# A hybrid diffusion layer on one core: the merge and the up-projection in hand-laid order on four engines

## The chip, the cores and the metric

One core of a Trainium2 chip runs the whole layer as one program. The metric is the device time of one execution, in microseconds (us). The engines are called as the profile calls them: PE (TensorE's matmuls; PEld its weight loads), DVE (VectorE), ACT (ScalarE), POOL (GpSimd) and SP (SyncE, which issues the DMAs here). Each engine takes its own instructions strictly in order, so an instruction that waits holds up all that stand behind it on that engine.

## The reference, cut to what matters

A layer with attention and a state-space part is followed by a merge and a feed-forward part. The change touches what follows after the attention output `attn` and the state-space output `ssm` are there:

```python
x = x + gate1 * (concat([rms_norm(attn, g_attn), rms_norm(ssm, g_ssm)]) @ w_out)   # the merge
h = rms_norm(x, g_norm2) * (1 + scale2) + shift2
up = h @ w_up                       # 1024 -> 5632 features
acc = conv3(up, conv_w) + conv_b    # centred, along the tokens, per feature
g, val = split(acc, 2)
x = x + gate2 * ((silu(g) * val) @ w_down)
y = rms_norm(x, g_final)
```

There are 128 prompt tokens and 2048 sample tokens, 2176 together (17 tiles of 128). All data are float32.

## The kernel before, in words

**Precision.** A float32 operand is split in two: ACT writes a rounded copy (hi), DVE or POOL subtracts it from the operand (lo), and three products hi·hi, hi·lo, lo·hi stand for one. So each operand of a matmul costs an ACT copy and a subtraction.

**The merge** (`merge`, L1016, in a loop over the 17 token tiles with two more passes of the loop behind them). The state-space half of each tile is turned by PE into the bank `to` and split into `oT` (`turned`, L974: copy L981, subtraction L982, square and sum L238 over `to`). 24 matmuls (tile `pm`, L280) are scaled, gated and added to x on DVE and POOL (`merge_ssm`, L1084 to L1086). `h2_begin` (L1092) takes the sum of squares of the finished row (ACT, L238), makes 1/rms on POOL (L239, L241) and scales to `xn` (DVE, L1109). In the next pass of the loop `h2_end` (L1112) turns `xn` into the banks `tp` (L1118), applies scale and shift with eight ACT instructions (L1121) and, for tokens from number 726 on, stores the result from the staging tile `stg` (two buffers) to the DRAM tensor `hd` (L1132). The square at L238 needs a place for its unused result, and `h2_begin` gives it the very `stg` tile that L1121 fills later. The last tile also clears six columns of its `stg` (MEMSET, L1106).

From pass 8 on the merge also prepares the feed-forward part: sums of token quarters on POOL (`sums0`, L1058), the split of token operands (`split_tokens`, L1181 copy, L1182 subtraction) and the first seven weight operands (`up_operands`, L1210 sums on POOL, L1215 copy, L1216 subtraction).

**The up-projection** (`ffn_up`, L1222) multiplies 2x2 blocks with seven products instead of eight. It makes three passes c = 0, 1, 2 over the tokens (726 each), each pass over 22 feature blocks fb, so 66 units. A unit has seven products of 12 matmuls of 366 columns: product 0 of the unit (the first one, `begin`, L1266, made ahead in the unit before), 1 into bank `Y`, 2 into `X`, 3 into `Z`, 4 into `X`, then product 0 of the next unit, 5 into `X`, 6 into `Z`. Between them ACT takes snapshots of the running bank `X` (`snap`, L1263: s1 before product 2, s2 before 4, s3 before 5), DVE adds snapshots to other banks (L1307, L1320, L1332), and the convolution is three taps (`taps`: ACT L1245, DVE L1246, L1247) on each of four results g1, v2, v1, g2. `silu` is an ACT tanh (L1253) and a DVE instruction (L1254); POOL multiplies (L1258, tile `th`) and SP stores to `ffd`. Meanwhile the weight operands of the next unit are made one by one (`step`): in pass 0 four sums on POOL, seven copies on ACT, six subtractions on DVE and one on POOL; in the passes 1 and 2 four of the seven come back from DRAM (`wsd`). `combos` makes the token combinations of the next pass on POOL; `operand` loads and splits them, two in unit fb = 18 and five in unit fb = 21.

**What sets the order.** Inside `tc.manual_schedule` an engine keeps the order of the code; elsewhere a scheduler chooses it by its own timeline. The merge is manual on PE, ACT, DVE and POOL, `ffn_up` on PE and POOL alone; SP is never manual here.

The down-projection (`ffn_down`, L1369) follows, in two halves of 11 blocks; `down_tile` and `down_early` load and split its first operands during the last two up units.

## Time and profile before

| what | us |
|---|---|
| median of 3 runs (2651.84 to 2657.8) | 2655.93 |
| the profiled execution | 2655.35 |
| its span, first to last instruction | 2653.6 |
| input projection, attention, state space | 0 to 980 |
| merge, until the first product of the up-projection | 980 to 1161 |
| up-projection: pass 0, pass 1, pass 2 | 1161 to 1515, to 1824, to 2135 |
| down-projection | 2135 to the end |

PE is busy for 2426.5 us of the span (91%), DVE 1738.3 (66%), ACT 1320.4 (50%) and POOL 1103.0 (42%). The granted clock of TensorE is given as a share of full speed (2.4 GHz): 1.00 where all of a stretch was at that level, 0.5 where all was at 1.2 GHz, and a mean between them; over the whole span it is 0.96. The shares are averages over stages with different limits; a stage is read by itself. A busy PE is the best sign of a stage that PE sets, since nothing else in these stages has to be as long as PE's own work.

### The profile page before, as it was taken

To read this page: it belongs to the slowest core of one execution; us is meant where nothing else is said; L and a number is where in the kernel's file an instruction comes from. 1 tells how busy PE (TensorE), PEld (TensorE's weight loads), DVE (VectorE), ACT (ScalarE), POOL (GpSimd) and SP (SyncE) were. 2 spreads that over 40 slices of the span, in tenths; PEclk is the share of its full clock that TensorE was granted. 3 is DMA by queue.
4 is the path that set the end of the run, shared out by engine and by line. 5 is a ranking of instruction groups with operands and counts; after the bars stand their busy time and mean duration, and the time that the engine had idled before them with its cause. 6 is when DMAs were issued, how large, how long until landed. Compare 5 with 4: busy or idle time off the path is not lost.

```text
span 2653.6 us, 38068 instructions
## 1 busy us (share of the span) xinstructions
PE 2426.5 (91%) x13294; PEld 2146.2 (81%) x13294; DVE 1738.3 (66%) x2979; ACT 1320.4 (50%) x2626; POOL 1103.0 (42%) x1393
## 2 busy tenths in 40 slices
PE   6986997799999779769998899999999999999998
PEld 3765785688887557569898899999999988888887
DVE  6999776877777876668888865567556542224333
ACT  6643557777776566555555644445444430112111
POOL 2686304577677725546666522232222221111101
PEclk8988998899999889879999999999999999999999
DMA  7554755421111657756777787788766763334432
GB/s 243 172 162 159 210 145 150 133 67 66 66 64 65 124 178 241 225 158 236 250 250 268 281 279 250 263 290 291 243 233 228 247 212 119 117 125 146 126 115 75
DMA packets 291039, 482.63 MB, mean 182 GB/s; under 512 B 42025, under 2 KB 187553, under 8 KB 290721
## 3 DMA queue, kind: packets, MB, share of 16 engines
q1 hardware_dynamic: 285953, 471.30, 54.6%
q10 hardware_dynamic: 4896, 8.92, 1.0%
q8 instruction: 105, 1.72, 0.3%
q14 instruction: 85, 0.70, 0.1%
HBM read 323.82 MB, written 153.95 MB: 180 GB/s over the span
## 4 chain that ended last, share of the span: by engine, by line
PE 56%; DVE 8%; issue 6%; ACT 5%; POOL 5%; DMA 4%; SPq 0%; POOLq 0%; DVEq 0%; ACTq 0%
PE dn L280 19%; PE X L1239 14%; PE Z L1239 7%; PE Y L1239 3%; PE pt L1009 3%; PE ps L858 2%; DMA hd<-stg 2%; POOL S L1210 2%; PE pt L886 2%; DVE w L1216 1%; PE pm L280 1%; ACT stg L1121 1%; PE po L890 1%; PE po L891 1%; DVE pTl L897 1%
## 5 line engine op out<-in xcount | busy, mean ns | idle before, releaser
L1239 PE MATMUL X<-T,w 128*128 128x366 f32 x3168 | 561.3, 332 | 30.6 <-ACT s L1263 27.5
L1239 PEld LDWEIGHTS X<-T,w 128*128 128x128 f32 x3168 | 536.3, 190 | 39.2 <-ACT s L1263 33.9
L1258 POOL TENSOR_TENSOR th<-th,v 128x363 f32<-128x363 f32 x132 | 139.6, 1058 | 550.1 <-issue 230.2
L1239 PE MATMUL Z<-T,w 128*128 128x366 f32 x1584 | 287.1, 330 | 3.3 <-DVE Y L1320 3.3
L280 PE MATMUL dn<-dnw,T 128*128 128x512 f32 (+1 forms) x1242 | 288.9, 386 | 0.0
L1239 PEld LDWEIGHTS Z<-T,w 128*128 128x128 f32 x1584 | 268.6, 189 | 4.2 <-DVE Y L1320 4.2
L280 PEld LDWEIGHTS dn<-dnw,T 128*128 128x128 f32 x1242 | 231.0, 188 | 47.0
L1408 DVE TENSOR_TENSOR td<-dn,gate 128x512 f32<-128x512 f32 (+1 forms) x69 | 47.1, 684 | 300.6 <-PE dn L280 300.6
L280 PE MATMUL dn<-T 128*128 128x512 f32 (+1 forms) x828 | 196.4, 386 | 0.0
L1347 ACT ACTIVATE T<-stg 128x1408 fp32r<-128x1408 f32 x34 | 47.1, 1385 | 281.0 <-PE dn L280 274.2
L280 PEld LDWEIGHTS dn<-T 128*128 128x128 f32 x828 | 154.0, 188 | 31.3
L194 DVE SCALAR_TENSOR_TENSOR wacc<-wa,scf,wacc 128x256 f32<-128x256 f32 x224 | 164.4, 778 | 12.8 <-ACT wacc L196 7.4
L1239 PE MATMUL Y<-T,w 128*128 128x366 f32 x792 | 143.8, 331 | 0.0
L897 DVE TENSOR_TENSOR pTl<-pt,pTh 128x512 fp32r<-128x512 f32 x158 | 108.1, 684 | 50.2 <-ACT pTh L896 48.6
L1263 ACT ACTIVATE s<-X 128x366 f32<-128x366 f32 x198 | 94.0, 475 | 93.2 <-PE X L1239 92.4
L239 POOL TENSOR_SCALAR ssq<-ssq 128x1 f32<-128x1 f32 x68 | 24.0, 353 | 269.7 <-ACT xn L238 91.9
L1239 PEld LDWEIGHTS Y<-T,w 128*128 128x128 f32 x792 | 134.9, 190 | 0.0
L1215 ACT ACTIVATE w<-upraw 128x512 fp32r<-128x512 f32 x198 | 121.9, 624 | 22.7 <-PE Z L1239 18.5
L624 POOL TENSOR_TENSOR fm<-HS,A 128x544 f32<-128x544 f32 x64 | 93.3, 1459 | 94.9 <-DVE HS L606 79.3
L860 DVE CUSTOM_DVE_ANT_0 sm<-ps,mask,nsink 128x640 f32<-128x640 f32 (+2 forms) x136 | 112.7, 830 | 28.9 <-PE ps L858 28.6
L1409 POOL TENSOR_TENSOR xd<-xd,td 128x512 f32<-128x512 f32 x34 | 46.5, 1371 | 197.5 <-DVE td L1408 191.6
L847 ACT ACTIVATE sm<-sm,nm 128x640 f32<-128x640 f32 (+2 forms) x136 | 107.6, 791 | 26.4 <-DVE nm L860 25.9
(493 smaller groups left out, 5498.6 us busy)
## 6 DMA issues: line engine op xcount, KB each, us to landing
w<-wsd SPq DMA_DIRECT2D x176, 512.0 KB, 5.1
upraw<-in_w_up_dram SPq DMA_DIRECT2D x88, 512.0 KB, 5.8
wsd<-w SPq DMA_DIRECT2D x88, 512.0 KB, 4.7
ffd<-th SPq DMA_DIRECT2D x132, 181.5 KB, 2.2
stg<-ffd SPq DMA_DIRECT2D x34, 704.0 KB, 4.8
xd<-x1d SPq DMA_DIRECT2D x34, 512.0 KB, 4.8
wa<-in_w_ada_dram SPq DMA_DIRECT2D x64, 256.0 KB, 3.0
upraw<-in_w_up_dram SPq DMA_DIRECT2D x44, 256.0 KB, 4.2
```

Of the source, the lines that this page charges most:

```text
L194: V.scalar_tensor_tensor(o, raw[:, k % RK], g, o, op0=OP.mult, op1=OP.add)
L280: self.T.matmul(ps, lhs(a, k), rhs(b, k), start=(first and k == 0 and n == 0), stop=(last and k == nk - 1 and n == 2))
L624: e.tensor_tensor(m, ev[:, :, ::-1] if n else ev, A[n], op=OP.mult)
L847: S.activation(out[hh][:, :W], out[hh][:, :W], AF.Exp, scale=-1.0, bias=nm[:, hh:hh + 1], accum_out=l[:, hh:hh + 1])
L858: T.matmul(ps[:, c:c + n], qT[:, h, :], kt, start=(a == 0), stop=(a == 1))
L860: V.tensor_tensor_reduce(t[:, :W], ps[:, c0:c0 + W], mask, -1.0, self.nsink[:, h:h + 1], op0=OP.add, op1=OP.min, accum_out=nm[:, hh:hh + 1])
L897: V.tensor_tensor(lo, pv, hi, op=OP.subtract)
L1009: T.matmul(pm, oT[:, a, k, :], w[:, b, k, cs], start=(n == 0), stop=(n == 11))
L1215: S.activation(w[:, 0], x, AF.Copy)
L1239: self.T.matmul(bank[:, :NI], w[:, a, k], t[:, b, k, :NI], start=(first and k + n == 0), stop=(k == 3 and n == 2), skip_group_check=True)
L1258: G.tensor_tensor(th, th, v, op=OP.mult)
L1263: S.activation(s[:, :NI], x[:, :NI], AF.Copy)
```

## The change

It does six things.

1. `h2_begin` gives the square the tile `xn` as its place for the unused result, in place of `stg`.
2. `ffn_up` and the merge stand in one manual order on PE, ACT, DVE and POOL. The code of `ffn_up` is written in the order wanted: the taps and silu of a unit's last result (g2) move behind product 1 and 2 of the next unit (`late`, `th2`).
3. The first product of the up-projection is made inside the merge, into a bank `X` of a pool of its own (three banks, `xp`); `to` has one bank in place of two and `tp` two in place of four. The fourth sum of quarters and the fourth token operand move into the merge too.
4. Loads of token operands are issued one or two units ahead of their splits (`load`, `split`), and the splits are spread over the units fb = 19, 20, 21 and 0 of the next pass.
5. In the passes 1 and 2 the second half of each token subtraction goes to POOL.
6. The loads of the first down operands are likewise issued ahead (`down_load`, `down_fetch`).

```diff
 def turned:   ps = pp.tile([128, 4, 128], F32, name="to", bufs=2 -> 1)
 def h2_end:   ps = pp.tile([128, 4, 128], F32, name="tp", bufs=4 -> 2)
...
     def merge(self, w, p, pp, xp):
             if 1 <= i <= NT:
                 hs[i - 1] = self.h2_begin(i - 1, xs.pop(i - 1), p)
+            if i == NT:
+                x = xp.tile([128, 512], F32, name="X", bufs=3)
+                self.product(wts[0], toks[0, 0], x, True)
             if i >= 2:
                 self.h2_end(i - 2, *hs.pop(i - 2), pp)
-            if i in (9, 11):
-                toks.append(self.split_tokens(len(toks), self.quarter(0 if i == 9 else 2)))
-            if 10 <= i < 16:
-                self.sums0((i - 10) // 2, slice(2 * (i % 2), 2 * (i % 2) + 2))
-            if i == 14:
-                toks.append(self.split_tokens(2, self.quarter(0)))
+            if i in (9, 11, 13):
+                j = len(toks)
+                toks[0, j] = self.operand0(j)
+            if 8 <= i < 16:
+                self.sums0((i - 8) // 2, slice(2 * (i % 2), 2 * (i % 2) + 2))
+            if i == NT:
+                toks[0, 3] = self.operand0(3)
...
     def h2_begin(self, i, x1, p):
-        r = self.rstd(x1.rearrange("p (k c) -> p k c", k=8), D, p, h[:, :, 0:128])
+        r = self.rstd(x1, D, p, xn)
...
     def split_tokens(self, n, src):
-            self.V.tensor_tensor(t[:, 1, k:k + 2, :NI], src[:, k:k + 2], t[:, 0, k:k + 2, :NI], op=OP.subtract)
+            e = self.G if k and n > 6 else self.V
+            e.tensor_tensor(t[:, 1, k:k + 2, :NI], src[:, k:k + 2], t[:, 0, k:k + 2, :NI], op=OP.subtract)
...
     def ffn_up(self, first, p, pp, xp):
+        banks = {0: (x0, snap(x0, "s1"))}
+        for j in range(4, 7):
+            toks[0, j] = self.operand0(j)
         for u, (c, fb) in enumerate(units):
...
             product(u, 1, y, True)
+            if late:
+                g2 = late()
+            step()
             V.tensor_tensor(y[:, :NI], y[:, :NI], s1[:, :NI], op=OP.add)
             product(u, 2, x)
             s2 = snap(x, "s2")
+            if late:
+                th2(g2)
             g1 = taps(y, 0, fb, "g1")
             t1 = silu(g1, y)
+            step()
+            if fb == 21:
+                split(c + 1, 3)
+                load(c + 1, 5)
+            if fb == 0:
+                split(c, 5)
...
             product(u, 3, z, True)
+            step()
+            if fb == 19:
+                split(c + 1, 0)
+                load(c + 1, 2)
             product(u, 4, x)
             s3 = snap(x, "s3")
             V.tensor_tensor(y[:, :NI], z[:, :NI], s3[:, :NI], op=OP.add)
+            step()
+            if u + 1 < len(units):
+                x1 = xp.tile([128, 512], F32, name="X", bufs=3)
+                product(u + 1, 0, x1, True)
             v2 = taps(y, 1, fb, "v2")
...
             product(u, 6, z)
             V.tensor_tensor(z[:, :NI], z[:, :NI], s2[:, :NI], op=OP.add)
-            g2 = taps(z, 0, fb, "g2")
-            gated(silu(g2, z), v2, 2 * c + 1, fb)
+            def late(z=z, fb=fb):
+                return taps(z, 0, fb, "g2")
+            def th2(g2, z=z, v2=v2, c=c, fb=fb):
+                gated(silu(g2, z), v2, 2 * c + 1, fb)
...
-            with self.pool("mrg2") as p, self.pool("mps2", bufs=2, space=PSUM) as pp:
-                with tc.manual_schedule(engines={ET.PE, ET.Activation, ET.DVE, ET.Pool}):
-                    first = self.merge(w, p, pp)
-            with fx, self.pool("upc") as p, self.pool("upps", space=PSUM) as pp:
-                with tc.manual_schedule(engines={ET.PE, ET.Pool}):
-                    self.ffn_up(first, p, pp)
+            xp = fx.enter_context(self.pool("upx", space=PSUM))
+            with tc.manual_schedule(engines={ET.PE, ET.Activation, ET.DVE, ET.Pool}):
+                with self.pool("mrg2", side="right") as p, self.pool("mps2", bufs=2, space=PSUM) as pp:
+                    steps = self.merge(w, p, pp, xp)
...
+                with fx, self.pool("upc") as p, self.pool("upps", space=PSUM) as pp:
+                    self.ffn_up(first, p, pp, xp)
```

Three places show the order. Names are tiles; a number behind a name tells one buffer from the next, and `x8` means eight in a row. The first place is PE at the end of the merge, before:

```order
L280 MATMUL pm<-wo,oT 128x512 x24
L1118 MATMUL tp<-ident,xn 128x128 x24
L1239 MATMUL X<-T,w 128x366 x12
L1239 MATMUL Y<-T,w 128x366 x12
L1239 MATMUL X<-T,w 128x366 x12
```

and in the changed kernel:

```order
L280 MATMUL pm<-wo,oT 128x512 x24
L1126 MATMUL tp<-ident,xn 128x128 x8
L1197 MATMUL X<-T,w 128x366 x12
L1126 MATMUL tp<-ident,xn 128x128 x16
L1197 MATMUL Y<-T,w 128x366 x12
L1197 MATMUL X<-T,w 128x366 x12
```

The first product (X) stands ahead of the last two tiles' transposes. The second place is POOL in one unit of pass 0, before (S are the four sums for the next unit's weights, w the one subtraction, th the two last products of a unit: first that of v1, then that of v2):

```order
L1216 TENSOR_TENSOR w<-upraw,w 128x512
L1258 TENSOR_TENSOR th<-th,v_13875 128x363
L1258 TENSOR_TENSOR th<-th,v_13836 128x363
L1210 TENSOR_TENSOR S<-upraw 128x512
L1210 TENSOR_TENSOR S<-S,upraw 128x512
L1210 TENSOR_TENSOR S<-upraw 128x512
L1210 TENSOR_TENSOR S<-upraw,S 128x512
```

and in the changed kernel:

```order
L1231 TENSOR_TENSOR w<-upraw,w 128x512
L1262 TENSOR_TENSOR th<-th,v_13875 128x363
L1225 TENSOR_TENSOR S<-upraw 128x512
L1262 TENSOR_TENSOR th<-th,v_13849 128x363
L1225 TENSOR_TENSOR S<-S,upraw 128x512
L1225 TENSOR_TENSOR S<-upraw 128x512
L1225 TENSOR_TENSOR S<-upraw,S 128x512
```

The second product of `th` changes places with the first sum. The third place is DVE in one unit of pass 0, before:

```order
L1320 TENSOR_TENSOR Y<-Z,s_14617 128x366
L1246 SCALAR_TENSOR_TENSOR v_14625<-Y,vec,v_14625 128x363
L1247 SCALAR_TENSOR_TENSOR v_14625<-Y,vec,v_14625 128x363
L1216 TENSOR_TENSOR w<-S,w 128x512 x2
L1246 SCALAR_TENSOR_TENSOR v_14664<-X,vec,v_14664 128x363
L1216 TENSOR_TENSOR w<-S,w 128x512
L1247 SCALAR_TENSOR_TENSOR v_14664<-X,vec,v_14664 128x363
L1332 TENSOR_TENSOR Z<-Z,s_14583 128x366
L1216 TENSOR_TENSOR w<-S,w 128x512
L1216 TENSOR_TENSOR w<-upraw,w 128x512 x2
L1307 TENSOR_TENSOR Y<-Y,s_14642 128x366
```

and in the changed kernel, from the add of the last product of a unit on:

```order
L1374 TENSOR_TENSOR Z<-Z,s_14103 128x366
L1231 TENSOR_TENSOR w<-S,w 128x512
L1250 SCALAR_TENSOR_TENSOR g_14237<-Z,vec,g_14237 128x363
L1251 SCALAR_TENSOR_TENSOR g_14237<-Z,vec,g_14237 128x363
L1231 TENSOR_TENSOR w<-upraw,w 128x512
L1316 TENSOR_TENSOR Y<-Y,s_14174 128x366
L1258 SCALAR_TENSOR_TENSOR th<-Z,g_14237 128x363
L1250 SCALAR_TENSOR_TENSOR g_14266<-Y,vec,g_14266 128x363
L1251 SCALAR_TENSOR_TENSOR g_14266<-Y,vec,g_14266 128x363
L1258 SCALAR_TENSOR_TENSOR th<-Y,g_14266 128x363
L1231 TENSOR_TENSOR w<-upraw,w 128x512
L1231 TENSOR_TENSOR w<-S,w 128x512
```

The six subtractions of weights, which stood in one cluster, now stand one or two at a time between the taps.

## Rows read from the trace of the kernel before

**Rows 1.** Windows: merge, merge body, merge end, pass 0, pass 1; PE, PEld, DVE, ACT, POOL, clock, DMA.

```profile
989.40:1050.94 61.54, 61.54 (x319) 51.97 (x317) 44.70 (x62) 36.95 (x91) 34.98 (x53) 0.98 0.78 263
1050.94:1133.94 83.00, 58.35 (x252) 45.73 (x250) 51.91 (x59) 43.40 (x103) 43.29 (x49) 0.84 0.79 218
1133.94:1186.44 52.50, 33.88 (x145) 30.65 (x146) 33.58 (x38) 29.90 (x64) 21.27 (x18) 0.69 0.55 171
1186.44:1515.23 328.79, 303.12 (x1766) 295.59 (x1765) 277.34 (x405) 183.74 (x342) 209.07 (x160) 0.99 0.70 248
1530.00:1790.00 260.00, 260.00 (x1557) 260.00 (x1556) 155.65 (x283) 124.16 (x226) 77.77 (x73) 1.00 0.78 268
```

**Rows 2.** Waits in 980 to 1165: us in total, times, longest.

```profile
ACT stg L238 <- DMA hd<-stg: 40.1, 9, 7.6
...
POOL ssq L239 <- ACT stg L238: 24.8, 10, 8.4
```

**Rows 3.** Chain that ended last, 1040 to 1165: start, us, what.

```profile
1094.03 7.06 DMA hd<-stg
...
1102.40 2.79 ACT stg L1121 x8
...
1150.04 5.13 DMA hd<-stg
```

**Rows 4.** Timeline of one token in the merge body: start, us, engine, instruction, [idle before].

```profile
1083.23 0.68 DVE L982 TENSOR_TENSOR oT<-to,oT 128x512 fp32r<-128x512 f32 x1
...
1086.73 1.82 POOL L1086 TENSOR_TENSOR mx__12116<-mx__12116,p 128x512 f32<-128x512 f32 x1
...
1090.44 0.19 POOL L239 TENSOR_SCALAR ssq<-ssq 128x1 f32<-128x1 f32 x1 [1.89 <-ACT stg L238]
...
1091.26 1.73 POOL L1058 TENSOR_TENSOR T<-T 128x732 f32<-128x732 f32 x1
1091.33 2.21 DVE L1109 TENSOR_SCALAR xn<-mx__12024,rstd 128x1024 f32<-128x1024 f32 x1 [3.92 <-POOL rstd L241]
...
1093.88 1.75 DVE L1182 TENSOR_TENSOR T<-T 128x732 fp32r<-128x732 f32 x2 [0.34 <-ACT T L1181]
```

**Rows 5.** Timeline of PE at the end of the merge.

```profile
1133.94 8.01 PE L280 MATMUL pm<-wo,oT 128*128 128x512 f32 x24 [3.19 <-ACT to L238]
...
1158.28 1.94 PE L1118 MATMUL tp<-ident,xn 128*128 128x128 f32 x8 [7.27 <-DVE xn L1109]
...
1164.84 2.77 PE L1239 MATMUL Y<-T,w 128*128 128x366 f32 x12
1171.69 4.03 PE L1239 MATMUL X<-T,w 128*128 128x366 f32 x12 [4.08 <-ACT s L1263]
```

**Rows 6.** Groups by line on DVE, 1200 to 1500: count, busy, mean ns, idle before.

```profile
L1216 DVE TENSOR_TENSOR w<-S,w 128x512 fp32r<-128x512 f32 x76 | 92.2, 1237 | 13.9 <-ACT w L1215 13.3
L1216 DVE TENSOR_TENSOR w<-upraw,w 128x512 fp32r<-128x512 f32 x38 | 31.9, 860 | 0.0
```

**Rows 7.** The same groups in pass 1, 1530 to 1790.

```profile
L1216 DVE TENSOR_TENSOR w<-upraw,w 128x512 fp32r<-128x512 f32 x36 | 24.9, 692 | 0.0
```

**Rows 8.** Timeline in pass 0: POOL's sums beside DVE's subtractions.

```profile
1246.10 1.28 POOL L1210 TENSOR_TENSOR S<-upraw 128x512 f32<-128x512 f32 x1
...
1246.84 2.79 DVE L1216 TENSOR_TENSOR w<-S,w 128x512 fp32r<-128x512 f32 x2 [1.85 <-ACT w L1215]
...
1247.34 1.75 POOL L1210 TENSOR_TENSOR S<-upraw,S 128x512 f32<-128x512 f32 x1
```

**Rows 9.** Timeline in pass 0: DVE idle between taps and silu, behind ACT.

```profile
1237.56 0.60 DVE L1246 SCALAR_TENSOR_TENSOR g<-Y,vec,g 128x363 f32<-128x363 f32 x1 [0.23 <-ACT g L1245]
...
1239.70 0.54 DVE L1254 SCALAR_TENSOR_TENSOR th<-Y,g 128x363 f32<-128x363 f32 x1 [0.60 <-ACT Y L1253]
...
1243.13 0.60 DVE L1246 SCALAR_TENSOR_TENSOR v<-X,vec,v 128x363 f32<-128x363 f32 x1 [0.29 <-ACT v L1245]
```

**Rows 10.** Waits in 1165 to 1510: us in total, times, longest.

```profile
POOL th L1258 <- DVE th L1254: 76.8, 19, 5.0
...
PE X L1239 <- ACT s L1263: 26.4, 18, 4.1
```

More of the change, by code (lines that the diff above doesn't have):

```diff
@@ L1047, in merge @@
                 wts = next(more)
-        return toks, wts, more, raws
+        for _ in more:
+            pass
+        yield toks, wts, raws, x
     def quarter(self, m):
@@ L1264, in snap, with load, split @@
             return s
-        def begin(u):
-            x = pp.tile([128, 512], F32, name="X", bufs=3)
-            product(u, 0, x, True)
-            banks[u] = x, snap(x, "s1")
-        todo, raws = [], first[3]
-        begin(0)
+        banks = {0: (x0, snap(x0, "s1"))}
+        todo, late, th2 = iter(()), None, None
+        for j in range(4, 7):
+            toks[0, j] = self.operand0(j)
+        raw = {}
+        def load(c, *js):
+            if 0 < c < 3:
+                for j in js:
+                    raw[j] = self.load_tokens(c, j)
+        def split(c, j):
+            if 0 < c < 3:
+                toks[c, j] = self.split_tokens(7 * c + j, raw.pop(j))
         for u, (c, fb) in enumerate(units):
             x, s1 = banks.pop(u)
-            nxt = iter(())
+            nxt, down = iter(()), u + 2 - len(units)
             if u + 2 < len(units):
@@ L1283, in ffn_up @@
                 next(todo)
+            z = pp.tile([128, 512], F32, name="Z", bufs=3)
             y = pp.tile([128, 512], F32, name="Y", bufs=2)
-            z = pp.tile([128, 512], F32, name="Z", bufs=3)
-            refill = fb == 21 and c < 2
-            def step(j):
-                for w in (next(nxt, None),):
-                    if w:
-                        wts[u + 1] = w
-                if refill and j is not None:
-                    toks[c + 1, j] = self.operand(c + 1, j)
-            if fb == 18 and c < 2:
-                for j in range(2):
-                    toks[c + 1, j] = self.operand(c + 1, j)
@@ L1298, in ffn_up, with step @@
-            if c == 2 and fb in (18, 19):
-                self.down_in.append(self.down_tile(0, fb - 18))
-            down = u + 2 - len(units)
-            if down >= 0:
-                self.down_early(down)
-            product(u, 1, y, True)
+            def step():
+                w = next(nxt, None)
+                if w:
+                    wts[u + 1] = w
+            if fb == 18:
+                load(c + 1, 0, 1)
+                if c == 2:
+                    downs = [self.down_load(0, i) for i in range(2)]
@@ new lines, in ffn_up @@
+            if down == 0:
+                self.down_fetch(0, 1)
+            if down == 1:
+                self.down_fetch(2, 3)
+            product(u, 1, y, True)
+            if late:
+                g2 = late()
+            step()
+            V.tensor_tensor(y[:, :NI], y[:, :NI], s1[:, :NI], op=OP.add)
+            product(u, 2, x)
+            s2 = snap(x, "s2")
+            if late:
+                th2(g2)
+            g1 = taps(y, 0, fb, "g1")
+            t1 = silu(g1, y)
+            step()
@@ L1304, in ffn_up @@
+            if down == 0:
+                self.down_early(0)
             if down == 1:
                 self.down_early(2)
[L1306 to L1314 removed]
+                self.down_fetch(5)
+            product(u, 4, x)
+            s3 = snap(x, "s3")
@@ new lines, in ffn_up @@
+            V.tensor_tensor(y[:, :NI], z[:, :NI], s3[:, :NI], op=OP.add)
+            step()
+            if u + 1 < len(units):
+                x1 = xp.tile([128, 512], F32, name="X", bufs=3)
+                product(u + 1, 0, x1, True)
+            v2 = taps(y, 1, fb, "v2")
+            if u + 1 < len(units):
+                banks[u + 1] = x1, snap(x1, "s1")
+            if fb == 20:
+                split(c + 1, 2)
+                load(c + 1, 4)
+            if fb == 21:
+                split(c + 1, 4)
+                load(c + 1, 6)
@@ L1315, in ffn_up @@
+            if fb == 0:
+                split(c, 6)
             if down == 1:
@@ L1317, in ffn_up @@
                 self.down_early(4)
-            product(u, 4, x)
-            s3 = snap(x, "s3")
-            V.tensor_tensor(y[:, :NI], z[:, :NI], s3[:, :NI], op=OP.add)
-            step(4)
-            v2 = taps(y, 1, fb, "v2")
-            if u + 1 < len(units):
-                begin(u + 1)
-            step(None)
+            step()
             product(u, 5, x)
-            step(5)
+            step()
+            if fb == 19:
+                split(c + 1, 1)
+                load(c + 1, 3)
             v1 = taps(x, 1, fb, "v1")
```

102 lines of the change are left out of this document (52 added, 50 removed).

## The prediction

> **What bounds the kernel now.** The windows by stage come first [rows 1]. In a stage that PE sets, PE's busy time is the stage. So it is in the merge before its pass 8 (61.54 of 61.54 us, nine tokens of 36 matmuls, 6.84 us each) and in pass 1 of the up-projection (260.00 of 260.00). Pass 1 also gives PE's price of a unit: 260 us for 1557 matmuls, 0.167 us each, 84 to a unit: 14.03 us. Three stretches are not PE's: the merge body (83.00 us for 252 matmuls, seven tokens, 11.86 us each, clock 0.84), the merge end (52.50 us with 33.88 of PE, clock 0.69) and pass 0 (328.79 us for 1766 matmuls, 21 units, 15.66 us each). The change touches these three, so each is read for the wait that ends last in it.
>
> In the merge the waits name a loop through memory [rows 2]: ACT's square at L238 waits nine times, 40.1 us, for a store out of `stg`, because `stg` takes the square's unused result; POOL then waits 24.8 us for the squares. The chain that ended last shows the same loop [rows 3]: a store lands (7.06), L1121 fills the tile again (2.79), the next store. In the tail the store that counts lands at 1150.04 + 5.13 = 1155.17.
>
> In pass 0 DVE is busy 277.34 of 328.79 us and POOL 209.07 [rows 1], neither full. The groups by line show why DVE is still in the way: a subtraction w takes 1.237 us (from a sum S) or 0.860 (from a raw weight) [rows 6], and 0.692 in pass 1, where POOL does little [rows 7]. The timeline shows the difference being made [rows 8]: POOL's sum starts at 1246.10 and ends 1247.38, the first of two subtractions starts inside it, at 1246.84; the two take 2.79 us, and the second ends at 1249.63, 0.54 behind the sum that POOL ran from 1247.34 to 1249.09. So a subtraction of DVE and an operation of POOL do not run beside each other: whichever comes second waits. Also, POOL's `th` waits for DVE's silu 76.8 us in pass 0 [rows 10], with the four sums in order behind it.
>
> **The change, part by part.** The profiled execution took 2655.35 us (span 2653.6), 0.6 below the median; the sums below are against it. About 0.2%, 5.3 us, is what a measurement can tell from no change.
>
> *Merge body.* With the square's result in `xn`, the wait of 40.1 us [rows 2] has no cause left, since `xn` is read by PE and stored by nobody. Late next is the in-order loop of DVE and POOL. In the token shown [rows 4] `oT` starts at 1083.23, the x add ends at 1088.55, ssq starts at 1090.44 after 1.89 us of waiting for the square, and `xn` at 1091.33: 8.1 us after `oT`. Without the wait that is 6.2; then `xn` (2.21), partly beside sums of POOL (1.73), and one weight subtraction of 0.7 to 1.5: 9.1 to 9.9 us a token, and 1.75 more in the passes with a token split. Measured is 11.86. The gain is best counted by POOL's waits: 24.8 less the longest, 8.4, which is the tail's, leaves 16.4. Two more sums of quarters (2 x 1.73) now fall on passes 8 and 9; I let them cost 1.4, since POOL idles there. **15 us.** Ends: 8, if half the waits are taken over by x add and sums, and 35, if PE sets the tokens (83.00 - 7 x 6.84).
>
> *Merge end.* Before, the last `pm` ends at 1133.94 + 8.01 = 1141.95 and product 2 of the first unit starts at 1171.69 [rows 5]: 29.7 us, with 7.27 of waiting for `xn`, then the products, then 4.08 for a snapshot that ACT makes behind other work. Now the first product runs while the last tiles are being normalised, and its snapshot stands ahead of the splits of the last three token operands. What stays is a store: the last tile's MEMSET clears part of a `stg` buffer whose store must have landed, and on DVE `xn` is queued behind it. That path from the end of `pm`: transposes 1.0, eight of L1121 2.79, issue 0.3, store 5.13 [rows 3]: 9.2; then MEMSET and `xn`, before 3.1 from landing to transpose (1155.17 to 1158.28) and now at most that; transposes 1.0 to 1.94 [rows 5], L1121 2.79 again, of which half can overlap with PE's next product. About 16. **14 us**, ends 8 (the store takes 7.06 and the splits are in the way) and 18.
>
> *Pass 0.* POOL no longer holds all its sums behind the second `th`: the first sum goes ahead of it. What remains is DVE's own work plus its meetings with POOL. Busy is 277.34 / 21 = 13.2 a unit; of this 4 x (1.237 - 0.692) + 2 x (0.860 - 0.692) = 2.5 is waiting inside subtractions, so 10.7 is work. Idle behind ACT, between taps and silu, is 0.23 + 0.60 + 0.29 = 1.1 [rows 9] and stays. Laying the new order of DVE beside POOL's with these durations, I find four meetings: the subtraction from raw weights with `th` (0.45), then three with the first, third and fourth sum (0.1, 1.0, 1.3): 2.85 in all. 10.7 + 1.1 + 2.85 = 14.65 a unit; 21 x (15.66 - 14.65) = 21. But the 328.79 also holds the combinations of tokens and the splits of the last units, which stay on POOL, DVE and ACT; I count half as real: **11 us**. The ends: 34, if no subtraction meets an operation of POOL (21 x 1.63, PE's floor), and 0. Six meetings with whole operations (6 x 1.3) would make it 19.6 a unit, 83 us lost; I exclude that, since POOL is busy 64% of the stage and a meeting costs on average half an operation.
>
> The rows settle the price of a meeting. The Trainium skill, page "SBUF — State Buffer", section "Who interferes with whom", says the same as a rule: a DVE instruction with two SBUF inputs and a GpSimd instruction that reads SBUF contend for one port pair, and it is "an exclusive lock". It speaks against this part of the change: spreading six subtractions between the taps exposes each of them to whatever POOL runs at that time, where the cluster of before met mainly the sums. By the rule taken at its worst the gain here is 0; the row-based count gives 11.
>
> *At nothing.* `to` with one bank and `tp` with two: PE waits for `xn` and ACT, not for banks, while tokens take over 9 us against 8.34 of PE (58.35 / 7). Operand loads ahead, POOL's halves of token splits in passes 1 and 2, and down loads ahead: behind PE, which is full there (260.00 of 260.00 [rows 1]), POOL having 77.77 us busy of 260; if that cover went, a unit boundary could lose some 2 us, twice. SP issues the same stores and loads, the loads earlier; a store of `th` behind a load costs nothing while POOL and DVE have buffers. The last unit has no product behind product 4, so product 5 waits for its snapshot: 1.5 at most.
>
> Sum: 15 + 14 + 11 = 40: **2615**.
>
> **The rivals.** *Faster, pass 0 at PE's floor.* If the subtractions fall into POOL's gaps, DVE needs 10.7 + 1.1 = 11.8 a unit, less than PE's 14.03, and PE is full: 15 + 14 + 34 = 63, 2592. For it: neither DVE (10.7 of work) nor POOL (209.07 / 21 = 10.0) needs PE's 14.03, and once PE sets the pace a short meeting is hidden. Against: with POOL at 10 us a unit, six subtractions hardly miss it all. 0.20.
>
> *The merge does not move.* The wait for the store turns up at L1121 itself, which fills the same two buffers, or POOL's chain of x add, ssq, pow and sums sets the pace as it stands; then only the 11 of pass 0 are left: 2644. For it: the store loop of 7.06 + 2.79 a token [rows 3] has nearly the token's time (11.86 for two buffers is ample, but one late landing shifts all). Against: at L238 the buffer is wanted one pass earlier than at L1121. 0.14; a third of this lies within 0.2%.
>
> *Slower, passes 1 and 2 lose PE.* They run at PE's pace now. The third snapshot stands on ACT behind the tanh of g1 and a weight copy, since ACT's order is now written out; and that tanh stands behind an add, a tap of ACT and two taps of DVE. Product 5 wants this snapshot; products 1 to 4 and the next unit's product 0 stand ahead of it on PE, so it is due 5 x 2.0 = 10.0 us after product 1 began. I find it done some 8.7 us after product 1 began, so 1.3 to spare. Every 0.1 us beyond that costs 44 units 4.4 us. It undoes the 40 at 0.9 us late; at 1.5 late it is 66 lost, 2681. Against: DVE is busy 155.65 of 260 us there, and ACT 124.16, so none of the queues is long [rows 1]. 0.08.
>
> **How the numbers follow.** The forecast has 0.58. The range runs from 2590 to 2644: it takes in the faster rival and the case of an unmoved merge, and the ends of the merge terms in ordinary combinations; the slower rival and the far ends are left out. Faster by over 0.2%: the forecast, the faster rival and two thirds of the unmoved merge, 0.87; within 0.2%: 0.06; slower: 0.07, nearly all of it the slower rival.
>
> **What the profile will show.** Right for the merge: no wait of ACT at L238 for a store, `xn` about 6 us after `oT`, tokens of 9 to 10.5 us, and DVE's MEMSET as the long wait at the end. Right for the merge end: about 16 us from the last `pm` to product 2. For pass 0 the unit's period decides: 14.03 (PE full, the faster rival), about 15 (forecast), 15.66 (nothing won), with the mean of the subtractions beside it, between 0.69 and 1.24. For passes 1 and 2: PE busy in all of 260 us; if PE waits for the third snapshot, the slower rival is true. The forecast fails if the tokens stay near 11.9, or if subtractions in pass 0 take over 1.3 each.

## The result and the profile after

The changed kernel takes 2627.69 us (median of 4 runs, 2625.28 to 2630.35) against 2656.54 of the kernel before: a ratio of 0.9895, 95% interval 0.9878 to 0.9912, 29 us less. The forecast was 2615 in a range of 2590 to 2644. The profiled execution took 2625.28 us, its span 2623.5, 30.1 less than before.

The windows by stage, cut at the same products as those of before [rows 1]; the columns are PE, PEld, DVE, ACT, POOL, clock, DMA share, GB/s:

```profile
986.55:1048.51 61.96, 61.96 (x318) 52.25 (x317) 44.41 (x62) 38.57 (x95) 35.04 (x53) 0.97 0.79 261
1048.51:1114.32 65.81, 54.41 (x252) 44.14 (x250) 51.16 (x59) 41.37 (x101) 46.51 (x51) 0.90 0.96 261
1114.32:1154.79 40.47, 29.84 (x148) 26.60 (x147) 26.38 (x35) 28.09 (x62) 16.65 (x18) 0.83 0.69 192
1154.79:1477.03 322.24, 307.12 (x1765) 301.93 (x1765) 284.84 (x402) 178.42 (x342) 210.84 (x164) 0.97 0.73 258
1492.85:1752.85 260.00, 260.00 (x1556) 260.00 (x1556) 161.26 (x278) 118.13 (x222) 77.49 (x73) 1.00 0.73 257
```

Against the same stretches of before this gives where the time went. A unit is counted from its product 1 (bank Y) to that of the next; the stretches outside the windows are taken from these starts.

| stretch | before | after | less | forecast |
|---|---|---|---|---|
| up to the merge body (program the same, or PE at its pace) | 1050.94 | 1048.51 | 2.4 | 0 |
| merge body, seven tokens | 83.00 | 65.81 | 17.2 | 15 |
| merge end, last `pm` to product 1 of the second unit | 52.50 | 40.47 | 12.0 | 14 |
| pass 0, 21 units | 328.79 | 322.24 | 6.6 | 11 |
| first unit of pass 1 | 14.05 | 15.82 | -1.8 | 0 |
| last unit of pass 1 and first of pass 2 | 30.96 | 34.35 | -3.4 | 0 |
| last two units and the down-projection | 545.5 | 548.5 | -3.0 | 0 |

So the three stages give 35.8 of the 40 forecast, and 8.2 is lost at places that the prediction had put at nothing. The 2.4 of the first line is no gain of the change: in the profiled executions of all runs, old code and new, the merge body starts anywhere from 1045.1 to 1050.9 us. How the merge parts into body and end also differs: in the six runs that leave the merge of the changed kernel as it is, the body takes 63.0 to 66.0 us, body and end together 105.7 to 106.4 (106.3 here, 135.5 before).

**The merge.** Of the two waits of before [rows 2] only one line with a store is left on ACT in the whole merge, and it is no longer at L238 (waits from 980 to 1136; us in total, times, longest):

```profile
ACT stg L1129 <- DMA hd<-stg: 4.4, 1, 4.4
...
DVE stg L1114 <- DMA hd<-stg: 0.7, 1, 0.7
```

The timeline of one token, to be read beside [rows 4]: `xn` starts 6.29 us behind `oT` (8.1 before; 6.2 was forecast), and the next `oT` follows 10.1 us behind this one (the seven tokens average 9.4), with a sum of POOL beside `xn` (1.76) and one beside the subtraction (1.73):

```profile
1083.60 0.68 DVE L982 TENSOR_TENSOR oT<-to,oT 128x512 fp32r<-128x512 f32 x1
...
1089.82 1.76 POOL L1066 TENSOR_TENSOR T<-T 128x732 f32<-128x732 f32 x1
1089.89 2.24 DVE L1117 TENSOR_SCALAR xn<-mx__12121,rstd 128x1024 f32<-128x1024 f32 x1 [2.11 <-ACT oT L981]
1091.54 1.73 POOL L1225 TENSOR_TENSOR S<-upraw 128x512 f32<-128x512 f32 x1
1092.05 1.76 DVE L1231 TENSOR_TENSOR w<-S,w 128x512 fp32r<-128x512 f32 x1
...
1093.73 0.68 DVE L982 TENSOR_TENSOR oT<-to,oT 128x512 fp32r<-128x512 f32 x1
```

At the merge end the MEMSET, which I had named as the long wait, waits 0.69 us. The long wait is ACT's L1129 of tile 15 (timeline, DVE and ACT):

```profile
1128.56 0.10 DVE L1114 MEMSET stg<- 128x48 f32 x1 [0.69 <-DMA hd<-stg]
...
1132.34 2.90 ACT L1129 ACTIVATE stg<-tp,modc,G 128x128 f32<-128x128 f32 x8 [4.43 <-DMA hd<-stg]
```

From the end of `pm` (1114.32 + 5.73 = 1120.05) to product 2 at 1139.87 it takes 19.8 us; before 29.7, forecast 16.

**Pass 0.** The groups by line on DVE, 1200 to 1440 (count, busy, mean ns, idle before), to be read beside [rows 6]:

```profile
L1231 DVE TENSOR_TENSOR w<-S,w 128x512 fp32r<-128x512 f32 x62 | 71.4, 1152 | 7.3 <-ACT w L1230 7.3
L1231 DVE TENSOR_TENSOR w<-upraw,w 128x512 fp32r<-128x512 f32 x32 | 37.4, 1168 | 0.2
```

The subtractions wait as long as before: 4 x 1.152 + 2 x 1.168 = 6.9 us a unit, where 6 x 0.692 + 2.85 = 7.0 was forecast. The ordinary units take 14.58 us (forecast 14.65), and 14.05 right behind a long one. But every fourth takes 18.2. PE's timeline in one of these:

```profile
1198.01 2.17 PE L1197 MATMUL Y<-T,w 128*128 128x366 f32 x12
...
1204.03 4.18 PE L1197 MATMUL X<-T,w 128*128 128x366 f32 x24
1210.53 2.84 PE L1197 MATMUL X<-T,w 128*128 128x366 f32 x12 [2.33 <-ACT s L1267]
...
1213.17 3.16 PE L1197 MATMUL Z<-T,w 128*128 128x366 f32 x12
```

These are the units fb = 4, 8, 12, 16, in which POOL makes four token combinations ahead of the first sum (timeline of POOL and ACT in the same unit):

```profile
1200.77 1.43 POOL L1153 TENSOR_TENSOR stg<-stg 128x366 f32<-128x366 f32 x1
...
1205.55 1.29 POOL L1225 TENSOR_TENSOR S<-upraw 128x512 f32<-128x512 f32 x1
...
1207.74 1.71 POOL L1225 TENSOR_TENSOR S<-S,upraw 128x512 f32<-128x512 f32 x1
...
1209.48 0.63 ACT L1230 ACTIVATE w<-S 128x512 fp32r<-128x512 f32 x1 [2.15 <-POOL S L1225]
```

The second sum comes late, ACT's copy of it waits 2.15 us, and the third snapshot, for which PE waits, stands behind that copy. The wait of 2.33 us is not all that the unit loses: the two products behind it take 2.84 and 3.16 us in place of 2.17, and the granted clock of the unit is 0.91. The run with the MEMSET late (below) shows the same unit with the same wait and the clock at 1.00; the product behind it takes 2.25. Windows of the unit here and there, and that product there:

```profile
1198.01:1216.17 18.16, 15.83 (x85) 15.53 (x85) 15.17 (x21) 9.36 (x18) 15.29 (x12) 0.91 0.92 311
1196.06:1212.68 16.62, 14.30 (x86) 14.00 (x85) 13.63 (x20) 9.08 (x18) 14.80 (x12) 1.00 0.91 315
...
1208.32 2.25 PE L1197 MATMUL X<-T,w 128*128 128x366 f32 x12 [2.32 <-ACT s L1267]
```

The unit behind takes 14.07 us here and 15.04 there, so over the two units the difference is 0.6 us (32.2 against 31.7).

### The profile page after: what moved, and what is told of

It is laid out like the page before. It is cut to its first block, busy times and chain, and to the rows that moved or that the text cites. A ratio compares the mean times of both kernels' runs of the same rounds, so it can differ in the third digit from the quotient of the medians.

```text
span 2623.5 us, 38108 instructions
## 1 busy us (share of the span) xinstructions
PE 2427.0 (93%) x13294; PEld 2148.9 (82%) x13294; DVE 1749.6 (67%) x2965; ACT 1305.9 (50%) x2626; POOL 1120.1 (43%) x1408
## 4 chain that ended last, share of the span: by engine, by line
PE 56%; DVE 11%; ACT 7%; issue 4%; DMA 4%; POOL 3%; SPq 0%; ACTq 0%; POOLq 0%; DVEq 0%
PE dn L280 19%; PE X L1197 13%; PE Z L1197 7%; PE Y L1197 4%; PE pt L1009 3%; PE ps L858 2%; PE pt L886 2%; DVE w L1231 2%; ACT w L1230 1%; PE po L890 1%; PE po L891 1%; DVE pTl L897 1%; ACT HS L606 1%; DVE ha L689 1%; DVE sm L860 1%
## 5 line engine op out<-in xcount | busy, mean ns | idle before, releaser
L1197 PE MATMUL Z<-T,w 128*128 128x366 f32 x1584 | 293.6, 335 | 4.1 <-DVE Y L1346 2.4
L1262 POOL TENSOR_TENSOR th<-th,v 128x363 f32<-128x363 f32 x132 | 129.4, 980 | 296.9 <-DVE th L1258 206.8
L1231 POOL TENSOR_TENSOR w<-upraw,w 128x512 fp32r<-128x512 f32 x66 | 89.4, 1354 | 248.7 <-DVE v L1251 141.6
```

The source lines that it names most:

```text
L1197: self.T.matmul(bank[:, :NI], w[:, a, k], t[:, b, k, :NI], start=(first and k + n == 0), stop=(k == 3 and n == 2), skip_group_check=True)
L1231: (G if n in WP7 else V).tensor_tensor(w[:, 1], x, w[:, 0], op=OP.subtract)
L1262: G.tensor_tensor(th, th, v, op=OP.mult)
```

## The experiments

| run | median, us | ratio to before, 95% interval |
|---|---|---|
| square in `stg` again | 2647.31 | 0.9973 (0.9964 to 0.9982) |
| kernel before, square in `xn` alone | 2630.98 | 0.9922 (0.9904 to 0.9939) |
| combinations spread, behind the third sum | 2626.78 | 0.9908 (0.9890 to 0.9926) |
| sums left out (a part of the computation is missing) | 2599.48 | 0.9797 (0.9783 to 0.9812) |
| third to fifth split of pass 2 later | 2620.93 | 0.9878 (0.9863 to 0.9892) |
| MEMSET late | 2620.66 | 0.9877 (0.9860 to 0.9893) |
| second sum ahead of `th` | 2601.55 | 0.9806 (0.9791 to 0.9820) |
| combinations spread, ahead of `th` | 2611.79 | 0.9845 (0.9830 to 0.9860) |
| first product behind the merge | 2624.33 | 0.9892 (0.9876 to 0.9909) |
| no halves of splits on POOL | 2621.48 | 0.9883 (0.9868 to 0.9898) |
| what helped, together | 2588.06 | 0.9756 (0.9742 to 0.9771) |

The kernel before had medians of 2653.2 to 2656.5 us in the sets of runs that these stand beside, so effects of a few us are read from the stages of the traces, each of which is one execution.

### The square's place: undone, and alone

```diff
-        r = self.rstd(x1, D, p, xn)
+        r = self.rstd(x1.rearrange("p (k c) -> p k c", k=8), D, p, h[:, :, 0:128])
```

> The changed kernel with one part undone: the square of h2_begin writes its unused result into the stg tile again. If the store wait was what held the merge body (theory), ACT waits at L238 for hd<-stg again, a token of the merge body takes over 11 us instead of about 10.4, and the run takes 2640 to 2652 us. If the hand-laid order and the first product in the merge won the time (rival), tokens stay near 10.4 us and the run stays within 5 us of the 2627.7 of the changed kernel.

> The kernel before with this part alone: the square's unused result goes to xn, nothing else is changed. Theory: the merge body loses its store wait, tokens of about 10.4 us instead of 11.9, some 15 to 24 us less in the merge, units of pass 0 as before (15.66 us on average): 2632 to 2642 us. Rival: the order around it keeps the token time (POOL's and DVE's chain was as long already), less than 6 us gained, over 2650 us.

Undone, the wait of [rows 2] is back (waits, 980 to 1136):

```profile
ACT stg L238 <- DMA hd<-stg: 35.0, 8, 7.2
```

and so is the time, 15.4 us in the merge body (81.21 against 65.81) and 7.1 in the merge end (47.57 against 40.47). Windows of body and end:

```profile
1047.32:1128.53 81.21, 59.98 (x251) 47.32 (x250) 51.32 (x59) 43.40 (x103) 46.49 (x51) 0.85 0.76 215
1128.53:1176.10 47.57, 29.70 (x145) 26.61 (x145) 27.38 (x35) 28.22 (x62) 16.36 (x17) 0.82 0.54 158
```

Alone, in the kernel before, the line brings the body to 66.06, as the whole change does, and the end to 47.30; pass 0 stays at 329.84:

```profile
1045.11:1111.17 66.06, 49.61 (x252) 39.73 (x250) 52.80 (x59) 41.30 (x101) 44.25 (x49) 0.99 0.95 272
1111.17:1158.47 47.30, 33.51 (x145) 30.35 (x145) 33.79 (x38) 29.73 (x64) 22.02 (x18) 0.76 0.62 190
1158.47:1488.31 329.84, 307.22 (x1766) 299.99 (x1766) 276.98 (x404) 183.49 (x342) 207.43 (x159) 0.98 0.69 247
```

Both times the theory holds (alone, with 2630.98 us, a little below the 2632 to 2642 expected): this one line is worth 20 to 23 us of the 29.

### The merge end: the MEMSET and the first product

```diff
 def h2_begin:
-            if i == NT - 1:
-                V.memset(h[:, :, 128:134], 0.0)
 def h2_end:
+        if i == NT - 1:
+            self.V.memset(h[:, :, 128:134], 0.0)
```

> The changed kernel with the MEMSET of the last tile moved behind the eight ACT instructions of the tile before it. Theory (a stg buffer goes to the instruction that first writes to it, so the early MEMSET took the buffer whose store was older, and tile 15 got the one of tile 14, whose store landed last): L1129 of tile 15 no longer waits 4.4 us, that of tile 16 waits at most 1, and product 2 of the first unit starts about 3 us earlier (from the end of pm 16.8 us instead of 19.8). Rival (the store of tile 14 is needed by one of the two tiles anyway): the wait moves to tile 16 with its size, product 2 starts within 0.5 us of now.

Product 2 now starts 16.5 us behind the end of `pm` (1115.41 + 5.70 = 1121.11 to 1137.63), 3.3 less, and the merge end takes 37.16. Tile 15 waits for its transposes and for no store, and tile 16 follows without a wait (ACT timeline):

```profile
1130.11 2.90 ACT L1129 ACTIVATE stg<-tp,modc,G 128x128 f32<-128x128 f32 x8 [1.28 <-PE tp L1126]
...
1134.28 2.93 ACT L1129 ACTIVATE stg<-tp,modc,G 128x128 f32<-128x128 f32 x8
```

So the theory holds. Since the square no longer writes `stg`, a tile's first write there is L1129, except for the last tile, whose MEMSET comes before L1129 of tile 15: the last tile took the buffer with the older store, and tile 15 the one with the newest.

```diff
-            if i == NT:
-                x = xp.tile([128, 512], F32, name="X", bufs=3)
-                self.product(wts[0], toks[0, 0], x, True)
...
         for _ in more:
             pass
+        x = xp.tile([128, 512], F32, name="X", bufs=3)
+        self.product(wts[0], toks[0, 0], x, True)
```

> The changed kernel with the first product of the up-projection put behind the transposes of the last tile, as in the kernel before. Theory (the product and its snapshot lie on the path that ends the merge): product 2 of the first unit starts 3 to 5 us later, 23 to 25 us after the end of pm instead of 19.8, about 2631. Rival (PE stands still there for L1129 and a store, and the snapshot is behind L1129 on ACT in any case): less than 1 us.

The rival holds. Product 2 starts 20.7 us behind the end of `pm`, 0.9 later, and by the second unit that is gone: the merge end takes 40.37 against 40.47. The first product in the merge is worth nothing here: in the changed kernel it ends at 1122.83 + 3.70 = 1126.5, but its snapshot stands on ACT behind L1129 of the last tile and starts at 1139.25.

### Pass 0: what a subtraction meets

```diff
-            s = self.upr.tile([128, 4, 512], F32, name="S", bufs=1)
+            if fb == 0:
+                self.s0 = self.upr.tile([128, 4, 512], F32, name="S", bufs=1)
+            s = self.s0
...
-            if c == 0 and n in sums:
+            if c == 0 and n in sums and fb < 2:
                 o, x0, x1, op = sums[n]
```

> The changed kernel without the four weight sums of POOL from the third unit of pass 0 on: the sums of an earlier unit are used in their place, so this part of the computation is left out and the time is only that of the rest. Theory (a subtraction of DVE that meets an operation of POOL waits for it, and this is all that keeps PE from its pace): the subtractions take 0.69 to 0.8 us on average instead of 1.13 and 1.19, units take 14.05, pass 0 is 20 to 27 us shorter, 2601 to 2608. Rival (DVE's waits for ACT between taps and silu hold the units): the subtractions become short all the same, but units stay at 14.5 or more and only the four long units gain, 2613 or more.

The theory holds: the 21 units take 299.07 us, nearly all of them 14.05, also those with combinations, and the means fall to 0.83 (a little more than expected) and 0.77 (groups on DVE, 1200 to 1440):

```profile
L1233 DVE TENSOR_TENSOR w<-S,w 128x512 fp32r<-128x512 f32 x67 | 55.5, 828 | 0.2 <-ACT w L1232 0.2
L1233 DVE TENSOR_TENSOR w<-upraw,w 128x512 fp32r<-128x512 f32 x34 | 26.2, 769 | 0.0
```

This run takes away the meetings and the waits for a sum together and does not tell them apart. Next, the same work in other places. First the second sum, moved ahead of the `th` of v2:

```diff
-            if c == 0 and n in sums:
-                o, x0, x1, op = sums[n]
+            for m0 in {0: (0, 1), 3: (3,), 5: (5,)}.get(n, ()) if c == 0 else ():
+                o, x0, x1, op = sums[m0]
                 G.tensor_tensor(o, x0, x1, op=op)
```

> The changed kernel with the second weight sum of POOL put ahead of the th product of v2, where POOL waits 1.5 us in each unit of pass 0. Theory (one meeting of a subtraction with a POOL operation fewer; the ordinary unit is 14.58 us because of the last one): the subtraction ahead of the add into Y is free, mean of the subtractions from 1.13 to about 1.0 us, ordinary units 14.05, some 6 to 9 us less, about 2620. Rival (the meeting moves to another subtraction): mean and units as they are, within 2 us of the changed kernel.

The direction was right and the size far too small: ordinary units take 14.05, and the long ones fell from 18.2 to 14.3, so that pass 0 takes 300.45 us, nearly as little as without any sums:

```profile
1153.69:1454.14 300.45, 296.92 (x1765) 294.70 (x1765) 269.54 (x402) 177.46 (x342) 214.26 (x164) 1.00 0.78 277
```

POOL is as busy as in the changed kernel (214.26 us, 210.84 there). In an ordinary unit of the changed kernel the last subtraction ahead of the add into Y ran into the fourth sum:

```profile
1239.90 1.75 POOL L1225 TENSOR_TENSOR S<-upraw,S 128x512 f32<-128x512 f32 x1
1240.41 1.78 DVE L1231 TENSOR_TENSOR w<-S,w 128x512 fp32r<-128x512 f32 x1
1242.12 0.53 DVE L1346 TENSOR_TENSOR Y<-Z,s 128x366 f32<-128x366 f32 x1
```

Now the fourth sum is over 0.5 us before that subtraction starts, and the subtraction takes 0.68:

```profile
1218.25 1.29 POOL L1225 TENSOR_TENSOR S<-upraw,S 128x512 f32<-128x512 f32 x1
...
1220.02 0.68 DVE L1231 TENSOR_TENSOR w<-S,w 128x512 fp32r<-128x512 f32 x1
1220.62 0.53 DVE L1346 TENSOR_TENSOR Y<-Z,s 128x366 f32<-128x366 f32 x1
```

The larger part of the 21.8 us, 15.4, comes from the four long units, and there for another reason: the second sum itself is done earlier, 9.1 us behind product 1 of the unit in place of 11.4, so ACT's copy of it waits 0.92 us in place of 2.15, and PE's wait of 2.33 is gone (ACT timeline of the first of these units, from 1195.83):

```profile
1204.98 0.63 ACT L1230 ACTIVATE w<-S 128x512 fp32r<-128x512 f32 x1 [0.92 <-POOL S L1225]
```

Two runs spread the combinations, one to a unit, and differ only in the place:

```diff
-            if fb in (4, 8, 12, 16) and c < 2:
...
+            if 2 <= fb < 18 and c < 2:
+                next(todo)
```

> The changed kernel with the sixteen token combinations of a pass on POOL issued one in each of the units 2 to 17, behind the third sum, where POOL then waits 3.2 us, instead of four at the start of each of the units 4, 8, 12, 16. Theory (POOL's block of four, 4.8 us ahead of the sums, makes the four units of 18.2 us): all units of pass 0 take 14.6 us, 4 x 3.6 = 14 us less, about 2613. Rival (DVE and POOL are full, so each combination only meets another subtraction): the sixteen units take 0.5 to 0.7 more each, of the 14 only 4 to 6 are left, about 2622.

> As the run with the combinations spread one to a unit, but each put behind the first sum and ahead of the th product of v2, where DVE runs taps (no subtraction) and POOL waits 1.5 us. Theory (it is not the amount of POOL's work but which DVE instruction runs beside it): the combination costs nothing there, the sixteen units take 14.6 to 14.8 instead of 15.5, total 12 to 14 us below the changed kernel, about 2614. Rival (POOL's order is the limit: everything behind the combination comes later by its 1.3 us): units of 15.2 to 15.6 again, about 2626.

Behind the third sum, the rival holds in its reason, and its size was too small: the sixteen units take 15.5 us, 0.9 more than the ordinary ones, and of the 14 us nothing is left; pass 0 takes 326.21, 4.0 more than in the changed kernel. One more subtraction meets POOL (mean from 1152 to 1400 ns):

```profile
L1241 DVE TENSOR_TENSOR w<-S,w 128x512 fp32r<-128x512 f32 x62 | 86.8, 1400 | 0.0
```

Ahead of `th`, where DVE runs taps, the theory holds: the sixteen units take 14.55 to 14.60 us, pass 0 takes 311.40, 10.8 less than in the changed kernel (12 to 14 were expected), and the mean is a little below the 1152 there:

```profile
L1241 DVE TENSOR_TENSOR w<-S,w 128x512 fp32r<-128x512 f32 x64 | 69.5, 1087 | 0.7 <-ACT w L1240 0.7
```

### The pass boundaries

In the changed kernel ACT stands 5.5 us in front of the third split of pass 2, whose buffer product 1 of the last unit still reads; the second snapshot comes late, and PE waits 1.96 us for it. The two products behind that wait take 5.82 us, where two without a wait took 4.18 above, and the granted clock of the unit is 0.91 (timeline):

```profile
1775.98 1.52 ACT L1188 ACTIVATE T<-stg 128x732 fp32r<-128x732 f32 x2 [5.54 <-PE Y L1197]
...
1781.92 5.82 PE L1197 MATMUL X<-T,w 128*128 128x366 f32 x24 [1.96 <-ACT s L1267]
```

```diff
             if fb == 21:
-                split(c + 1, 3)
-                load(c + 1, 5)
+                split(c + 1, 2 if c else 3)
+                load(c + 1, 4 if c else 5)
...
+            if fb == 21 and c == 1:
+                split(2, 4)
+                load(2, 6)
```

> The changed kernel with the third to fifth token splits of pass 2 moved half a unit to a unit later, so that the third stands behind product 1 of the last unit of pass 1, the last reader of the buffer it fills. Theory (ACT stood 5.5 us in front of that split, and the snapshots behind it came late): the units 43 and 44, now 18.5 + 15.8 us, take 30 to 32 together, 2 to 4 us less in all. Rival (five splits in two units are what costs, wherever they stand): the later splits hold up the products of unit 44, the two units together stay at 33.5 to 35.

The rival holds in its number, not in its reason: the units 43 and 44 take 14.04 + 20.77 = 34.8 us, the wait only moved. It is now a load that ACT waits for, because with two raw buffers the later splits issue their loads later:

```profile
1789.38 1.52 ACT L1188 ACTIVATE T<-stg 128x732 fp32r<-128x732 f32 x2 [5.62 <-DMA stg<-td]
```

```diff
-            e = self.G if k and n > 6 else self.V
+            e = self.V
```

> The changed kernel with both halves of each token split of the passes 1 and 2 on DVE, as before. Theory (POOL's half relieves DVE at the pass boundaries): the boundary units 20 to 22 and 43 to 44 get longer by 1 to 4 us in all. Rival (POOL takes 1.8 us for what DVE does in 0.9, and product 6 of the units 22 and 44 waits for POOL's half): these units get shorter by 1 to 2 us in all, the rest is equal.

Neither theory nor rival is shown: the four units from fb = 19 on take 65.4 us and the units 43 and 44 34.7, against 63.8 and 34.3 of the changed kernel; but with POOL's halves kept, the run with the late MEMSET shows 65.4 for the first four as well. POOL's halves are worth 0.4 us at most at the second boundary, and nothing that stands out at the first.

### What helped, together

```diff
 def load_tokens(self, p, j, spare=False):
+        if spare:
+            raw = self.upr.tile([128, 4, 512], F32, name="S", bufs=1)[:, :, :NI]
...
-        for j in range(4, 7):
-            toks[0, j] = self.operand0(j)
+        toks[0, 4] = self.operand0(4)
...
+            if fb == 21 and c == 1:
+                split(2, 2)
+                load(2, 5)
+            if fb == 0 and c:
+                split(c, 5)
...
             s3 = snap(x, "s3")
             V.tensor_tensor(y[:, :NI], z[:, :NI], s3[:, :NI], op=OP.add)
+            if down == 1:
+                self.down_early(1)
...
```

Besides the two edits already shown, the operands (1, 5), (2, 2) and (2, 5) are loaded into the tile S; pass 2 has its splits 0 and 1 in fb = 19, 2 to 4 in fb = 21, 5 and 6 in fb = 0; pass 0 has its splits 5 and 6 behind the snapshot of product 2.

> The changed kernel with what the runs so far have shown to help: the second sum ahead of th (22.9 us in the profile, pass 0 at 14.05 and 14.32), the late MEMSET (3.3 us at the merge end), and new: a third buffer for operand loads (the sums' tile S, which is free behind pass 0), so that the splits of the units 21 to 44 stand where their data and buffers are there, the last two splits of pass 0 behind the snapshot of product 2, and the early splits of the down-projection behind the third snapshot of the last unit. Theory (the boundary units are long because splits wait on ACT for buffers and loads): units 20 to 22 and 43 to 44 together 4 to 10 us shorter, unit 0 by 1 to 2, the last unit by 1 to 2; total 2587 to 2596. Rival (the boundaries cost what five splits of ACT and DVE take): only the sum of the two shown gains, 2598 to 2602.

The theory holds: 2588.06 us, 65 less than the kernel before in the same set of runs (2653.17) and faster than both kernels of this study. The windows of the merge end and of pass 0:

```profile
1114.79:1150.97 36.18, 27.76 (x148) 24.83 (x145) 27.41 (x35) 27.82 (x62) 16.83 (x18) 0.91 0.78 230
1150.97:1451.39 300.42, 296.90 (x1765) 294.68 (x1765) 269.81 (x402) 177.76 (x343) 214.58 (x164) 1.00 0.77 277
```

The units 43 and 44 take 14.04 + 14.46 us (34.35 in the changed kernel), the first unit 17.78 (18.73), the last two units with the down-projection 545.4 (548.5). With a third raw buffer the five splits of these two units wait for no load there and 0.25 us at most for a reader, so it was the waits that cost at this boundary, with the lower clock behind them, not the work of five splits.

## Why the prediction held, and where it did not

The time lay in the range, on the side of a smaller gain: 29 us instead of 41 from the median.

**Merge body, 15 forecast, 17.2 measured.** The mechanism is shown by both runs on the square: the wait at L238 goes, and the loop of DVE and POOL takes its place at 9.4 us a token (65.81 / 7; the prediction had 9.1 to 9.9). The chain that ended last shows the change of hands: before, from 1053 to 1101, it goes in turn over stores and ACT, L1121 above all; now, from 1054 to 1085, it is on POOL and DVE, with gaps and 0.6 us on ACT. Counting POOL's waits came out 2 short.

**Merge end, 14 forecast, 12.0 measured.** The size is near, and in part by luck, for the working was wrong in two steps. The step by which the last tile's MEMSET waits for a store, "and on DVE `xn` is queued behind it", failed: the buffers went the other way round, and L1129 of tile 15 had the wait, at a price of 3.3 us. And of the first product in the merge, which the step counted as part of the gain, nothing is left when it is undone; 5.2 (alone) to 7.1 us (undone) belong to the square. Two of the 12 us are not waits: the last `pm` took 8.01 us in the kernel before [rows 5] and 5.73 now, the granted clock of the stretch being 0.69 and 0.83. In the merge end the whole change gains 6.8 us over the square alone (47.30 to 40.47): 2.8 in the last `pm` (8.56 to 5.73), 2.9 in the first unit (21.60 to 18.73) and 1.1 between them; which of its parts gave the 2.9 was not tested. The sum's 0.3 for issuing a store has no row: before, L1121 ends at 1147.23 + 2.80 and the store starts at 1150.04. As the merge parts into body and end differently from execution to execution, the safer number is the sum of both terms, 29.2 against 29.

**Pass 0, 11 forecast, 6.6 measured.** The count of meetings was right: 6.9 us of subtractions a unit against 7.0, units of 14.58 against 14.65. In the unit from 1230.24 the four that were forecast are there, with `th`, the first, the third and the fourth sum: they cost 0.55, 0.18, 0.73 and 1.09 us over the 0.69 of a subtraction alone (forecast 0.45, 0.1, 1.0, 1.3), and each of these subtractions ends 0.54 or 0.55 us behind the operation of POOL that it met. The term was mis-sized where I "count half as real" for the combinations and the splits: the block of four combinations ahead of the sums makes units of 18.2, and of the 21 us that the ordinary units alone would have given more than two thirds went there and to the units fb = 19 to 21 (15.25, 17.76 and 15.01). The runs on pass 0 show the meeting and its price: one subtraction takes 1.78 us with a sum beside it and 0.68 without, and a combination costs 0.9 us a unit beside subtractions and nothing beside taps, which take one of their two tensor inputs from PSUM. The Trainium skill, page "SBUF — State Buffer", section "Who interferes with whom", gives this as a rule: a DVE instruction with two SBUF inputs contends with a GpSimd instruction that reads SBUF, and one with at most one SBUF input, outside the 2-port modes, does not. These runs agree with it.

**At nothing, minus 8.2 measured.** This is the step that failed most. Its ground, "behind PE, which is full there", was read from the middle of pass 1; at the ends of a pass PE waits, in three places for three reasons. In the first unit of pass 1 (1.8 lost), where the split of the last token operand now stands, product 6 waits for it:

```profile
1490.29 1.28 PE L1197 MATMUL Z<-T,w 128*128 128x366 f32 x6 [0.59 <-DVE T L1190]
```

At the second boundary (3.4) ACT's order is now fixed, and a split that waits for a reader holds up the snapshots behind it. In the last unit (3.0, with the down-projection) ACT waits for nothing: two copies for the down-projection, 1.99 us, stand ahead of the third snapshot, and PE waits for that (the down-projection then waits 1.73 us for DVE):

```profile
2097.17 1.99 ACT L1410 ACTIVATE T<-upraw 128x1024 fp32r<-128x1024 f32 x2
...
2099.58 2.28 PE L1197 MATMUL X<-T,w 128*128 128x366 f32 x12 [1.61 <-ACT s L1267]
```

The losses of 1.8 and 3.4 stand against "some 2 us, twice" in the prediction and the 3.0 against "1.5 at most", but both stood outside its sum. Nor is all of the 3.4 the change's. In the run with the square alone, whose code is that of the kernel before there, the same two units take 14.62 + 18.96 = 33.6 us, 2.6 more than in the profiled execution of the kernel before. Behind a wait of 2.0 us that both have, the product takes 3.79 us there and 2.26 in the other, which is 1.5 of the 2.6:

```profile
1813.29 3.79 PE L1239 MATMUL Z<-T,w 128*128 128x366 f32 x12 [2.01 <-DVE Y L1320]
```

**The rivals.** The fast one, pass 0 at PE's floor, is not what the change does, but one sum moved in POOL's order nearly makes it true (300.45 us against 21 x 14.05 = 295). Not that the subtractions then miss POOL, they still take 1.03 us on average there; it is the prediction's other reason, that a short meeting is hidden once PE sets the pace. The unmoved merge is out: ACT's waits for a store fell from 40.1 to 4.4 us. The slow one was excluded for the right reason: in pass 1 the third snapshot ends 8.7 us behind product 1 (1549.03 to 1557.74), as estimated, and PE is busy 260.00 of 260.00:

```profile
1557.26 0.48 ACT L1267 ACTIVATE s<-X 128x366 f32<-128x366 f32 x1 [0.21 <-PE X L1197]
```

Still open: why the granted clock falls behind a wait of 2.3 us in some of the long units (18.2 us) and not in others (16.6), and which of the edits of the last run shortened the first boundary.

## What to carry to other kernels

Look for a scratch operand that shares a buffer with something that a DMA still reads: here one such line was worth 20 to 23 of 29 us. Where DVE and POOL both read SBUF, ask which instructions run at the same time, not only how much work there is: the sixteen combinations cost 0.9 us a unit beside DVE's subtractions and nothing beside its taps, which read PSUM. In an order written by hand, each instruction that can wait for a buffer or a load is a wait for all behind it, so boundaries have to be read and costed by themselves.

## What was not expected

- One sum moved by one place on POOL took 22 us out of 21 units (322.24 to 300.45): the meeting of 1.1 us that it removed gave the ordinary units 0.5 each, and the sum's earlier end gave the four long units 3.9 each.
- The order in which instructions first write to tiles decides which buffer each gets: an early MEMSET of 0.10 us cost 3.3.
- A wait of PE can cost more than its length: behind about 2 us of standing still the granted clock of a unit was 0.91 in some places and 1.00 in others, and at 0.91 the products behind the wait took up to 1.7 us more. The merge end, too, had a higher granted clock where it was shorter (0.69, 0.83, and 0.91 with the MEMSET late), but what raised it there was not tested.
